# Gate weights split once and kept: a hybrid S5 and RWKV-7 block on one core

## The chip, the cores and the metric

The kernel runs on one core of one Trainium2 chip. The metric is the device time of one execution in microseconds (us). Each execution profiled below has a span (first to last instruction of the program) and a time a little above it. The engines are TensorE (PE in the profile; its weight loads are PEld), VectorE (DVE), ScalarE (ACT), GpSimd (POOL) and SyncE (SP), which here only issues DMAs.

## The reference

One trunk layer on 2048 frames of 1024 features, in float32:

```python
h = rmsnorm(x, norm1_g)
proj = h @ w_in                       # [u | p_rwkv | gate_a | gate_b], 512+1792+1024+1024 columns
gate_a, gate_b = sigmoid(proj[..., s2:s3]), sigmoid(proj[..., s3:])
o_a = s5_branch(u, ...)               # diagonal complex state-space model and half-GLU
o_b = rwkv7_branch(p_rwkv, ...)       # 8 heads x 64, delta-rule recurrence over the frames
merged = gate_a * (o_a @ wb[:512]) + gate_b * (o_b @ wb[512:])
x = x + merged @ w_out
x = x + square(relu(rmsnorm(x, norm2_g) @ w_ff1)) @ w_ff2
return rmsnorm(x, norm_f_g)
```

The change concerns the product of h with the last 2048 columns of w_in, the gate weights.

## The kernel before, in words

Large products are made in three passes (`mm3`, lines 120 to 123): each float32 operand is split into a high part rounded to float32r and a low part, the rest, and TensorE adds high x low, low x high and high x high. The parts come from a copy that rounds (ScalarE as a rule) and a subtraction of the rounded from the raw (GpSimd or VectorE).

The program runs in phases. Phase A makes h, writes its two parts to memory (`h_d`), and projects the RWKV and S5 inputs. Phase B, about 540 to 1400 us, holds two things at once:

- The RWKV recurrence, in 16 chunks of 128 frames: `elem` (elementwise preparation), `inv` (inverse of a triangular matrix per head; its 16 x 16 blocks go through memory in 8 KB transfers, lines 783 to 787, are worked on in the loop of lines 802 to 809 on VectorE, and come back at lines 810 to 816; `X` of line 817 is then what TensorE needs) and `chain` (the state, serial over the chunks).
- `gates`, which makes the gate columns: four quarters `w` of 512 frames; in each the parts of h come from `h_d` (16 tiles, line 969), then 16 strips `m` of 128 columns, 24 matmuls each. `loadw(m)`, called one strip ahead, loads strip m's weights (512 KB, line 955), copies them to the high part `gwh` (ScalarE, line 958) and subtracts to the low part `gwl` (GpSimd, line 959). All this is done anew in each quarter, 64 times in all. The weight tiles alternate between two pools, so a strip's weights lie where those of two strips before lay. The result goes through ScalarE (line 985) and a store that is issued a strip late (line 986) to `gt_d`.

`robin` (line 82) takes a step of `chain`, `gates`, `elem` and `inv` in turn until the chunk's work is done; `gates` goes on into the next chunk. This sets the program order. The framework then orders each engine's instructions by this order and its own model of when each becomes ready, except those pinned with `keep_in_program_order`, and sets the waits. Each engine and each queue of DMA issues runs in the order so found. Nearly all DMAs of phase B are issued by SyncE. `Late` holds back a given number of actions: with `Late()` an action runs when the next one is put.

Phase C (branch outputs, gates applied from `gt_d`, output projection) and phase D (the feed-forward part) follow.

Of the kernel before, what the change touches and what calls it, by code (L numbers as in the profile page):

```python
# [10 lines left out]
F32 = mybir.dt.float32  # L11
# [10 lines left out]
NK = DM // 128  # L22
# [97 lines left out]
def mm3(nc, ps, wh, wl, xh, xl, start, stop):  # L120
    nc.tensor.matmul(ps, wh, xl, start=start, stop=False)  # L121
    nc.tensor.matmul(ps, wl, xh, start=False, stop=False)  # L122
    nc.tensor.matmul(ps, wh, xh, start=False, stop=stop)  # L123
# [473 lines left out]
        weave(dense(), s5_stream(tc, nc, K, io, R, u_d, z_d, sp, pss), ratio=2)  # L597


def phase_b(tc, nc, K, io, pm_d, ob_d, h_d, gt_d, inv_d):  # L600
    V, A, P, T = nc.vector, nc.scalar, nc.gpsimd, nc.tensor
    NS = S // 128
    with ExitStack() as st:
# [343 lines left out]
            D[s] = None  # L947

        def gates():
            late = Late()  # L950

            def loadw(m):
                pool = (gw, gt)[m % 2]
                wr = pool.tile([128, NK, 128], F32, tag="wr", name=f"gwr{m}")
                nc.sync.dma_start(wr, io["win"][18 + m % 16])
                wh = pool.tile([128, NK, 128], F32R, tag="wh", name=f"gwh{m}")
                wl = pool.tile([128, NK, 128], F32R, tag="wl", name=f"gwl{m}")
                A.copy(wh, wr)  # L958
                P.tensor_tensor(wl, wr, wh, op=ALU.subtract)  # L959
                return wh, wl  # L960

            nxt = loadw(0)
            for w in range(NW):
                hs = []
                for k in range(NK):
                    r = []
                    for i in range(2):
                        t = (gw if k < 5 else gt).tile([128, 512], F32R, tag=f"h{i}{k}", name=f"gh{w}_{i}{k}")
                        nc.sync.dma_start(t.bitcast(F32), h_d[i, w, :, k, :])
                        r.append(t)  # L970
                    hs.append(r)
                for _ in range(5):
                    yield
                for m in range(16):
                    wh, wl = nxt
                    j = 16 * w + m
                    if j + 1 < 16 * NW:
                        nxt = loadw(j + 1)
                    pp = psd.tile([128, 512], F32, tag="d", name=f"gp{j}")
                    for k in range(NK):  # L980
                        mm3(nc, pp, wh[:, k], wl[:, k], hs[k][0], hs[k][1], k == 0, k == NK - 1)
                        if k % 2 and k < NK - 1:
                            yield
                    sg = gt.tile([128, 512], F32, tag="sg", name=f"gs{j}", bufs=2)
                    A.copy(sg, pp)
                    late.put(lambda m=m, w=w, sg=sg: nc.sync.dma_start(
                        gt_d[128 * m:128 * m + 128, 512 * w:512 * w + 512], sg))
                    yield
            late.flush()

        gg = Side(gates())
        next(gg)
        for i in range(NS + 2):
# [733 lines left out]
def ff_open(tc, nc, K, io, x1_d, xt_d, r_d, st):  # L1727

    rp = st.enter_context(tc.tile_pool(name="e_r", bufs=1, reuse_waits="tile"))
    s1 = ExitStack()  # L1730
    return s1, FF1(tc, nc, K, io, x1_d, xt_d, r_d, s1, rp)


def phase_d(tc, nc, K, io, x1_d, r_d, out, s1, ff):
    pieces = a_pieces(nc, io, r_d, ff.tile4)
    w2 = {}

    def w2raw(g):
        if g not in w2:
            w2[g] = {}  # L1740
            for j in range(2):
                for l in range(2):
                    t = ff.tile4(2 * j + l, f"w2{g}_{j}{l}")
                    m = 4 * g + 2 * j
                    nc.sync.dma_start(t, io["w2"][m:m + 2, :, 512 * l:512 * l + 512].rearrange("b p n -> p b n"))
                    w2[g][j, l] = t
        return w2[g]

    def start():
        w2raw(0)  # L1750
        for n in range(4):
            pieces[1](n)

    with s1:
        ff.run(s1, start)
    phase_d2(tc, nc, K, io, x1_d, out, pieces, w2raw, ff.tile4)


def setup(tc, nc, st, io):
    K = Net()  # L1760
    cp = st.enter_context(tc.tile_pool(name="glob", bufs=1))
    ca = cp.tile([128, NCST_A], F32, name="csta")
    nc.sync.dma_start(ca, io["cst"][:, 0:NCST_A])
    vec = cp.tile([128, NVEC], F32, name="vec")
    nc.sync.dma_start(vec, io["vec"])
    K.ident = ca[:, 0:128]
    K.r7 = ca[:, 128:144]
    K.mhalf = cp.tile([128, 1], F32, name="mhalf")
    nc.gpsimd.memset(K.mhalf, -0.5)
    K.ss = cp.tile([128, 2, 16], F32, name="ss1")  # L1770
    K.rq = cp.tile([128, 16], F32, name="rq1")
    K.vec = lambda n: vec[:, VOFF[n]:VOFF[n] + VEC_N.get(n, 4)]
    return K
# [34 lines left out]
@with_exitstack  # L1808
def tile_hybrid_block(ctx: ExitStack, tc: tile.TileContext, io: dict, out: bass.AP):
    nc = tc.nc  # L1810
    dp = ctx.enter_context(tc.tile_pool(name="dram", bufs=1, space=DRAM))
    u_d = dp.tile([512, 8, S // 8], F32, name="u_d")
    pm_d = dp.tile([2688, S], F32, name="pm_d")
    gt_d = dp.tile([2 * DM, S], F32, name="gt_d")
    h_d = dp.tile([2, NW, 128, NK, WT], F32, name="h_d")
    inv_d = dp.tile([S // 128, 2, 64, 256], F32, name="inv_d")
    z_d = dp.tile([512, 8, S // 8], F32, name="z_d")
    ob_d = dp.tile([512, S], F32, name="ob_d")
    oa_d = dp.tile([512, S], F32, name="oa_d")
    x1_d = dp.tile([S, DM], F32, name="x1_d")  # L1820
    xt_d = dp.tile([3, 2, 128, 4, 512], F32, name="xt_d")
    r_d = dp.tile([16, 4, 128, 2, 512], F32, name="r_d")
    if True:
        K = setup(tc, nc, ctx, io)
        phase_a(tc, nc, K, io, u_d, pm_d, h_d, z_d)
        phase_b(tc, nc, K, io, pm_d, ob_d, h_d, gt_d, inv_d)
        with ExitStack() as sd:
            ff = []

            def following():  # L1830
                ff.extend(ff_open(tc, nc, K, io, x1_d, xt_d, r_d, sd))
                return ff[1].ahead()

            phase_c(tc, nc, K, io, z_d, oa_d, ob_d, gt_d, x1_d, xt_d, following)
            phase_d(tc, nc, K, io, x1_d, r_d, out, *ff)
# [21 lines left out]
```

## Time and profile before

| | |
|---|---|
| median of 3 runs | 3114.84 us (3110.07 to 3119.49) |
| profiled execution: time, span | 3106.43 us, 3104.7 us |
| mean granted TensorE clock | 0.970 |
| busy of the span: TensorE, VectorE, GpSimd, ScalarE | 94%, 63%, 43%, 38% |
| line 955, loads of raw gate weights | 64 x 512 KB, 3.7 us to landing (median) |
| line 986, stores of gate columns | 64 x 256 KB, 2.8 us to landing (median) |

How to read it: a group's row gives line, engine, operation, what is written and read, the count, then busy us and the mean ns of one, then the engine's idle time before it and what ended that. In a row of waits stand the total us, the number of waits and the longest. In a window's row each engine's busy us is followed by its count of instructions; then come the granted clock, the DMA engines' busy share and GB/s. A tile's or line's row gives minimum/median/maximum in ns, and the first and last start in us. A row in order of time gives start and duration in us, and in brackets the idle time before and what ended it. In instruction names `x<-y` is what is written and what is read. A busy TensorE is not one at its peak, and some matmul records can be missing.

### The profile page before, as it was taken

The page shows a single profiled execution, that of the slowest core. Times are in us where ns is not written, and L with a number is a line of the kernel's source. Part 1 is how long each engine was busy: PE and PEld are TensorE (multiplying, and loading weights), DVE is VectorE, ACT ScalarE, POOL GpSimd, SP SyncE. Part 2 cuts the span into 40 slices and gives each one's busy share as a digit, 9 for nine tenths or more (in the row PEclk, how much of TensorE's full clock was granted, in tenths as well). Part 3 has the DMA queues.
Part 4 walks back from the last instruction along what each step waited for, and adds up shares of the span by engine and source line. Part 5 has one row for each costly group of instructions (what it writes and reads, how often), then busy time and mean ns, then how long its engine had stood idle before and what let it go on. Part 6 is the DMA issues. An engine that isn't in the chain of part 4 may idle for free.

```text
span 3104.7 us, 45582 instructions
## 1 busy us (share of the span) xinstructions
PE 2928.6 (94%) x17024; PEld 2339.1 (75%) x17024; DVE 1942.6 (63%) x3307; ACT 1164.4 (38%) x1843; POOL 1333.7 (43%) x1117
## 2 busy tenths in 40 slices
PE   7989999589899999998999999999999999999998
PEld 5757777367677767777777878887788888888887
DVE  5348875367877777745333266656755566666667
ACT  4441211234343344324444455555333442222233
POOL 3100100645555455422433335555444655555564
PEclk9999999789899999999999999999999999999999
DMA  4344444534435334228656664333533386666664
GB/s 148 96 134 136 137 142 136 180 100 128 127 98 159 92 97 144 77 92 241 194 182 185 197 200 153 109 109 106 176 111 113 97 271 153 151 153 153 154 145 148
DMA packets 320157, 444.10 MB, mean 143 GB/s; under 512 B 112064, under 2 KB 173632, under 8 KB 319936
## 3 DMA queue, kind: packets, MB, share of 16 engines
q1 hardware_dynamic: 291776, 401.34, 40.6%
q0 software_dynamic: 11520, 35.66, 6.7%
q10 hardware_dynamic: 16640, 4.20, 0.5%
q8 instruction: 134, 2.20, 0.3%
q14 instruction: 87, 0.71, 0.1%
HBM read 302.55 MB, written 131.07 MB: 140 GB/s over the span
## 4 chain that ended last, share of the span: by engine, by line
PE 46%; DVE 5%; DMA 4%; issue 2%; POOL 2%; ACT 1%; SPq 0%; POOLq 0%; ACTq 0%; DVEq 0%
PE s L122 6%; PE s L123 6%; PE s L121 6%; PE f L121 5%; PE f L123 5%; PE f L122 5%; DMA wor<-in_wout_dram 1%; DMA g<-gt_d 1%; PE b L121 1%; PE b L122 1%; PE b L123 1%; PE o L121 1%; PE o L122 1%; PE o L123 1%; DVE bl L1318 1%
## 5 line engine op out<-in xcount | busy, mean ns | idle before, releaser
L121 PE MATMUL f<-bl,w1h 128*128 128x512 f32 x896 | 355.5, 397 | 8.9 <-ACT w1h L1345 8.9
L122 PE MATMUL f<-bh,w1l 128*128 128x512 f32 x896 | 351.8, 393 | 3.7 <-POOL w1l L1349 3.7
L123 PE MATMUL f<-bh,w1h 128*128 128x512 f32 x896 | 352.6, 394 | 0.0
L122 PE MATMUL s<-w2h,al 128*128 128x512 f32 x784 | 305.5, 390 | 1.0 <-POOL al L1563 1.0
L123 PE MATMUL s<-w2h,ah 128*128 128x512 f32 x784 | 305.4, 390 | 0.0
L121 PE MATMUL s<-w2l,ah 128*128 128x512 f32 x784 | 305.4, 390 | 0.0
L1349 POOL TENSOR_TENSOR w1l<-w1r,w1h 128x512 fp32r<-128x512 f32 x122 | 174.7, 1434 | 185.1 <-ACT w1h L1345 184.6
L121 PE MATMUL gp<-gh,gwh 128*128 128x512 f32 x512 | 228.8, 447 | 10.9 <-DMA gh<-h_d 10.8
L122 PE MATMUL gp<-gh,gwl 128*128 128x512 f32 x512 | 214.8, 420 | 6.4 <-POOL gwl L959 6.4
L1345 ACT CAST w1h<-w1r 128x512 fp32r<-128x512 f32 x224 | 137.7, 620 | 205.9 <-PE f L123 150.1
L1563 POOL TENSOR_TENSOR al<-ra,ah 128x1024 fp32r<-128x1024 f32 x64 | 167.4, 2617 | 108.0 <-ACT ah L1562 107.8
L123 PE MATMUL gp<-gh,gwh 128*128 128x512 f32 x512 | 211.1, 412 | 0.0
L1593 DVE TENSOR_TENSOR c<-c,s 128x512 f32<-128x512 f32 x224 | 149.9, 684 | 90.2 <-PE s L123 90.0
L121 PEld LDWEIGHTS f<-bl,w1h 128*128 128x128 f32 x896 | 169.8, 190 | 44.8 <-ACT w1h L1345 9.9
L122 PEld LDWEIGHTS f<-bh,w1l 128*128 128x128 f32 x896 | 169.6, 189 | 43.7 <-POOL w1l L1349 7.2
L123 PEld LDWEIGHTS f<-bh,w1h 128*128 128x128 f32 x896 | 169.3, 189 | 38.2
L959 POOL TENSOR_TENSOR gwl<-gwr,gwh 128x1024 fp32r<-128x1024 f32 x64 | 153.7, 2401 | 97.5 <-ACT gwh L958 81.8
L121 PE MATMUL p<-hl,wh 128*128 128x512 f32 x448 | 182.8, 408 | 3.6 <-ACT lo L583 3.6
L123 PE MATMUL p<-hh,wh 128*128 128x512 f32 x448 | 178.5, 399 | 0.0
L122 PE MATMUL p<-hh,wl 128*128 128x512 f32 x448 | 178.1, 398 | 0.0
L122 PEld LDWEIGHTS s<-w2h,al 128*128 128x128 f32 x784 | 147.3, 188 | 31.7 <-POOL al L1563 1.4
L123 PEld LDWEIGHTS s<-w2h,ah 128*128 128x128 f32 x784 | 147.3, 188 | 30.5
(382 smaller groups left out, 6995.1 us busy)
## 6 DMA issues: line engine op xcount, KB each, us to landing
gwr<-in_win_dram SPq DMA_DIRECT2D x64, 512.0 KB, 3.7
w1r<-in_w_dram SPq DMA_DIRECT2D x64, 512.0 KB, 3.4
r_d<-c SPq DMA_DIRECT2D x128, 256.0 KB, 2.0
ra<-r_d SPq DMA_DIRECT2D x64, 512.0 KB, 3.5
ch<-r_d POOLq DMA_DIRECT2D x42, 512.0 KB, 5.8
gh<-h_d SPq DMA_DIRECT2D x64, 256.0 KB, 5.0
gt_d<-gs SPq DMA_DIRECT2D x64, 256.0 KB, 2.8
g<-gt_d SPq DMA_DIRECT2D x64, 256.0 KB, 3.4
```

The source lines that it names most:

```text
L121: nc.tensor.matmul(ps, wh, xl, start=start, stop=False)
L122: nc.tensor.matmul(ps, wl, xh, start=False, stop=False)
L123: nc.tensor.matmul(ps, wh, xh, start=False, stop=stop)
L959: P.tensor_tensor(wl, wr, wh, op=ALU.subtract)
L1318: V.tensor_tensor(l[k], o, h[k], op=ALU.subtract)
L1345: cast = A.copy(h, o)
L1349: (P if n % 2 or edge else V).tensor_tensor(l, o, h, op=ALU.subtract)
L1563: P.tensor_tensor(l, raw[n], h, op=ALU.subtract)
L1593: V.tensor_tensor(d, d, bank, op=ALU.add if i in (4, 5, 6) else ALU.subtract)
```

## The change

In the first quarter, as before, each strip's weights are loaded raw and split. Now both parts are also stored to a new tensor in memory, `gs_d` (16 strips x 2 parts x 512 KB), one strip late; the last strip's at the last strip of the quarter. In the other three quarters both parts are loaded from `gs_d` straight into the tiles that the matmuls read, with no copy and no subtraction. The values are the same bits.

```diff
-def phase_b(tc, nc, K, io, pm_d, ob_d, h_d, gt_d, inv_d):
+def phase_b(tc, nc, K, io, pm_d, ob_d, h_d, gt_d, gs_d, inv_d):
...
         def gates():
-            late = Late()
+            late, keep = Late(), Late()
 
             def loadw(m):
+
                 pool = (gw, gt)[m % 2]
-                wr = pool.tile([128, NK, 128], F32, tag="wr", name=f"gwr{m}")
-                nc.sync.dma_start(wr, io["win"][18 + m % 16])
                 wh = pool.tile([128, NK, 128], F32R, tag="wh", name=f"gwh{m}")
                 wl = pool.tile([128, NK, 128], F32R, tag="wl", name=f"gwl{m}")
+                if m >= 16:
+                    for e, t in enumerate((wh, wl)):
+                        nc.sync.dma_start(t.bitcast(F32), gs_d[m % 16, e])
+                    return wh, wl
+                wr = pool.tile([128, NK, 128], F32, tag="wr", name=f"gwr{m}")
+                nc.sync.dma_start(wr, io["win"][18 + m])
                 A.copy(wh, wr)
                 P.tensor_tensor(wl, wr, wh, op=ALU.subtract)
+
+                def store():
+                    for e, t in enumerate((wh, wl)):
+                        nc.sync.dma_start(gs_d[m, e], t.bitcast(F32))
+
+                keep.put(store)
                 return wh, wl
...
                     j = 16 * w + m
+                    if j == 15:
+                        keep.flush()
                     if j + 1 < 16 * NW:
                         nxt = loadw(j + 1)
...
+    gs_d = dp.tile([16, 2, 128, NK, 128], F32, name="gs_d")
...
-        phase_b(tc, nc, K, io, pm_d, ob_d, h_d, gt_d, inv_d)
+        phase_b(tc, nc, K, io, pm_d, ob_d, h_d, gt_d, gs_d, inv_d)
```

## The prediction, made before the changed kernel was run

> **What bounds the kernel now.** I read the stage table first (busy time of each engine in chosen stretches), then the list of waits on TensorE, then the groups of VectorE instructions, and last the order of time around single stalls. The edited code runs in one stage, from 540 to 1400 us. There TensorE works through 64 gate strips (24 matmuls each), four quarters of 16, woven with the RWKV recurrence. The edit spares work in quarters two to four, 760 to 1400 us, and adds stores in the first, 540 to 760 us.
>
> ```profile
> core 0: us, PE busy (x) PEld busy (x) DVE busy (x) ACT busy (x) POOL busy (x), PEclk, DMA share, GB/s
> 540.00:760.00 220.00, 171.01 (x1440) 132.35 (x1439) 129.58 (x228) 69.55 (x113) 125.64 (x138) 0.85 0.44 133
> 760.00:1400.00 640.00, 591.99 (x5973) 460.02 (x5971) 457.23 (x833) 235.58 (x380) 304.76 (x309) 0.94 0.38 113
> 1700.00:1800.00 100.00, 100.00 (x460) 82.71 (x459) 30.67 (x43) 44.32 (x82) 37.01 (x30) 1.00 0.63 195
> ```
>
> In quarters two to four TensorE is busy 592 of 640 us and its granted clock is 0.94, against 1.00 in a later stage without stalls. So 48 us are idle, and 6% of 640, 38 us, is clock not granted. ScalarE and GpSimd are half idle or more; sparing them time is worth nothing by itself. What TensorE waits for is this:
>
> ```profile
> engine line waited for: us in total, times, longest us
> PE P L667 <- DVE X L817: 14.4, 5, 5.2
> PE bo L745 <- DVE ys L944: 11.7, 3, 4.6
> PE U L899 <- DVE Rs L895: 8.1, 4, 4.5
> ...
> PE gp L122 <- POOL gwl L959: 0.6, 1, 0.6
> ```
>
> The gate weights themselves make TensorE wait 0.6 us (the last row). The other three rows, 34.2 us, are waits for VectorE, and nearly all of the small rows left out are too (46 us with them). So the question is why VectorE is late, and whether the removed work has a part in it. It has:
>
> ```profile
> 921.86 4.42 DVE L934 TENSOR_TENSOR ys<-ys,y 128x512 f32<-128x512 f32 x1
> ...
> 922.12 2.38 POOL L959 TENSOR_TENSOR gwl<-gwr,gwh 128x1024 fp32r<-128x1024 f32 x1
> 924.47 1.26 POOL L746 TENSOR_TENSOR BK<-km,e 128x512 f32<-128x512 f32 x1
> ...
> 929.84 1.44 PE L667 MATMUL P<-X,TM 64*64 64x64 f32 x22 [5.19 <-DVE X L817]
> ...
> 927.00:933.80 6.80, 3.96 (x37) 3.28 (x37) 5.69 (x7) 1.57 (x3) 4.54 (x3) 0.50 0.82 231
> ...
> L934 DVE TENSOR_TENSOR ys<-ys,y x14: 645/693/4420, 780.0 to 1385.3; 128x512 f32<-128x512 f32 x14
> ```
>
> The VectorE multiply at L934 has a median of 0.69 us. Beside the gate weights' subtraction on GpSimd (L959) and the next GpSimd operation it took 4.42 us and ended when the second did. The X of L817 behind it came late, TensorE waited 5.19 us for it, and its clock stood at 0.50 for 6.8 us (last window row). That is one case; groups and both ends of the list show how common it is:
>
> ```profile
> L805 DVE TENSOR_TENSOR yt<-NC,YC 64x15 f32<-64x15 f32 (+7 forms) x195 | 70.2, 360 | 13.6 <-DMA NC<-inv_d 8.3
> L807 DVE TENSOR_TENSOR YC<-YC,yt 64x15 f32<-64x15 f32 (+7 forms) x195 | 56.6, 290 | 5.7
> L934 DVE TENSOR_TENSOR ys<-ys,y 128x512 f32<-128x512 f32 x14 | 18.9, 1354 | 0.3
> L717 DVE TENSOR_TENSOR AR<-rm,e 128x512 f32<-128x512 f32 x11 | 17.0, 1547 | 9.3 <-ACT e L706 9.1
> ...
> L805 DVE TENSOR_TENSOR yt<-NC,YC x195: 116/206/2841, 765.1 to 1343.8; 64x15 f32<-64x15 f32 x26, 64x28 f32<-64x28 f32 x26, 64x39 f32<-64x39 f32 x26, 64x48 f32<-64x48 f32 x26
> L807 DVE TENSOR_TENSOR YC<-YC,yt x195: 101/206/2392, 765.3 to 1344.0; 64x15 f32<-64x15 f32 x26, 64x28 f32<-64x28 f32 x26, 64x39 f32<-64x39 f32 x26, 64x48 f32<-64x48 f32 x26
> L717 DVE TENSOR_TENSOR AR<-rm,e x11: 647/694/6431, 759.5 to 1241.3; 128x512 f32<-128x512 f32 x11
> ...
> 765.97 2.30 DVE L805 TENSOR_TENSOR yt<-NC,YC 64x39 f32<-64x39 f32 x1
> 765.85 2.37 POOL L959 TENSOR_TENSOR gwl<-gwr,gwh 128x1024 fp32r<-128x1024 f32 x1
> ...
> 1341.45 2.35 DVE L807 TENSOR_TENSOR YC<-YC,yt 64x28 f32<-64x28 f32 x1
> 1341.37 2.39 POOL L959 TENSOR_TENSOR gwl<-gwr,gwh 128x1024 fp32r<-128x1024 f32 x1 [3.15 <-ACT gwh L958]
> ```
>
> Mean minus median, times count: L805 (360-206) x 195 = 30.0 us, L807 16.4, L934 9.3, L717 9.4: 65 us of VectorE time lost beside GpSimd. 22 VectorE instructions, the first and the last of them in the four rows above, were each stretched by at least 1.8 us beside one L959. So L959's share is at least 22 x 1.8 = 40 us, at most these 65 and what smaller groups add.
>
> **The change part by part.** The profiled execution took 3106.4 us; the median of the runs, 3114.84, is 8.4 above it. I work out a difference and apply it to both.
>
> Removed in quarters two to four, 48 times each: the ScalarE copy, the GpSimd subtraction and the 512 KB load of raw weights.
>
> ```profile
> L958 ACT CAST gwh<-gwr x64: 1027/1049/1069, 548.6 to 1389.4; 128x1024 fp32r<-128x1024 f32 x64
> L959 POOL TENSOR_TENSOR gwl<-gwr,gwh x64: 2332/2380/2850, 549.7 to 1390.5; 128x1024 fp32r<-128x1024 f32 x64
> L955 SPq DMA_DIRECT2D gwr<-in_win_dram x46: 328/351/1654, 789.3 to 1377.6; - x46
> DMA to landing us min/median/max: 3.1/3.8/5.6
> ```
>
> *ScalarE*: 48 x 1.05 = 50 us of an engine busy 236 of 640; I count nothing. *GpSimd*: 48 x 2.38 = 114 us off, and with it the 40 to 65 us of VectorE. What TensorE gets of that: I followed the unbroken run of VectorE work back from each of the 21 stalls of 0.4 us or more that VectorE ended between 760 and 1400 us, and took, stall by stall, the smaller of the stall and the time stretched beside L959 in that run. It sums to 33 us. The stalls at 1307.72 (2.51 us) and 1352.76 (2.27 us) get nothing: the run ahead of them is short and begins at a transfer's landing. Bounds: 0, if other waits fill the place, and all 46 us. I take 33.
>
> *The clock*: 38 us not granted follow such stalls. With 33 of 47 us of stalls gone I take 70% back, 27 us, and 0.6 of that as work really paced by the clock (the rest is small matmuls and idle time): 16 us. Bounds 0 and 38.
>
> *Added in the first quarter*: 32 stores of 512 KB, from SyncE's queue. No row has such a store; the 256 KB ones of L986 issue in 0.34 us and land in 2.5, so 32 x 0.34 = 11 us of queue time, on an engine that mostly waits. Bounds 0 to 11; I take 3, since each is issued a strip late and GpSimd has ended by then; behind it stand the small transfers of the inverse.
>
> *Added afterwards*: two 512 KB loads per strip in place of one, and a new wait: they write where strip m-2's weights lie, so SyncE waits for that strip's last matmul. Now it waits only for L959, and loads far ahead:
>
> ```profile
> 799.75 0.35 SPq L955 DMA_DIRECT2D gwr<-in_win_dram  x1
> 812.51 0.34 SPq L986 DMA_DIRECT2D gt_d<-gs  x1
> ...
> 811.90 0.59 ACT L985 COPY gs<-gp 128x512 f32<-128x512 f32 x1 [0.54 <-PE gp L123]
> ...
> 1394.40 0.59 ACT L985 COPY gs<-gp 128x512 f32<-128x512 f32 x1 [3.95 <-issue]
> 1399.84 0.59 ACT L985 COPY gs<-gp 128x512 f32<-128x512 f32 x1 [4.85 <-PE gp L123]
> ...
> SPq L986 <- ACT gs L985: 132.0, 30, 11.1
> SPq L955 <- POOL gwl L959: 86.4, 31, 7.8
> ```
>
> The load of strip 20 went out at 799.75, 12 us before strip 17 ended (its L985 copy is at 811.90). The edited load can go out only at the end of strip 18. SyncE already waits there 30 times for the copy that follows the same matmul (L986, 132 us), and the instruction order is planned anew by the framework's own model of readiness, so I expect the new wait beside that one and L955's 86 us gone. The pair of loads then has one strip's time to land: between 3.8 us (both at once) and 0.35 + 2 x 3.8 = 8.0 (one after the other). A strip takes 640/48 = 13 us on average, but the last, without recurrence beside them, 5.4 (1394.40 to 1399.84). Some four short strips could be late by up to 2.6 us: 0 to 10 us, I take 3. By the Trainium skill ("DMA: Bandwidth & Descriptors", section Bandwidth) a 1 MB load takes 6.15 us, which would make it 3 us by an estimate; no run here shows the pair yet.
>
> *Small transfers*: the inverse's 8 KB transfers share the queue with the loads.
>
> ```profile
> L814 SPq DMA_DIRECT2D Y<-inv_d x104: 313/429/1032, 778.9 to 1350.0; - x104
> ```
>
> 104 of them are 13 chunks of eight. An extra load issued ahead costs 0.35 us and some data time; bounds 0 and one extra microsecond on each of 13 chunks; I take 5.
>
> Sum: -33 - 16 + 3 + 3 + 5 = -38 us. 3106.4 becomes 3068 for the profiled execution, 3114.8 becomes 3077 for the median.
>
> **The rivals.**
> *Hidden.* VectorE is freed and only waits longer for TensorE and for the inverse's round trip. For it: the two stalls without any stretched work, 2.4 us each. If each of 13 chunks keeps such a stall, 31 of 47 us remain, 16 go, the clock gives nothing, costs 11: -5, 3110. Against it: most stalls have 2 us or more of stretched work just ahead.
>
> *Slower.* SyncE's queue: the gate loads wait for the strip's end, and the inverse's transfers (L783, L810, L814), ready by then, stand behind them; VectorE's chain gets its blocks late and TensorE waits for X. The nearest price is L986's wait, 132/30 = 4.4 us. Once in each of 13 chunks: +57 - 38 = +19, 3134. It decides from 38/13 = 2.9 us a chunk. Against it: the L986 wait is in the queue already.
>
> *More.* All 46 us of VectorE stalls go and 0.6 of the 38 us of clock, with 5 of costs: -64, 3051. A rule speaks for it: the Trainium skill ("TensorE: Matmul & The Clock Gate", section HAM oscillation) asks only that no idle gap exceed about 3.4 us, so short stalls that are left would cost no clock. The rows disagree:
>
> ```profile
> 1051.91 0.80 PE L667 MATMUL P<-X,TM 64*64 64x64 f32 x20 [1.79 <-DVE yt L805]
> ...
> 1053.30:1056.70 3.40, 3.40 (x37) 2.49 (x35) 2.09 (x10) 0.39 (x1) 0.00 (x0) 0.50 0.00 1
> ```
>
> A stall of 1.79 us was followed by 3.4 us at half clock.
>
> **How the numbers follow.** Forecast 0.61, hidden 0.15, slower 0.12, more 0.12. The forecast's own range, from the bounds of the clock, the costs and a new instruction order, is 3055 to 3105. The 8-in-10 range takes in most of the other cases: 3046 to 3118. About 0.3%, 9 us, is what a measurement can tell from no change. Faster than that: nearly all of forecast and more, and a quarter of hidden: 0.75. Slower 0.12. Within: 0.13.
>
> **What would show it.** In the changed trace: L805 and L807 means near 0.25 us from 760 us on; TensorE's waits for VectorE there near 14 us and its clock near 0.98; the stage some 40 us shorter, everything after it the same length. Wrong if SyncE's waits for TensorE come to stand ahead of L783 or L810, if TensorE waits for the loaded weights in more than a few strips, or if VectorE's means stay up because other GpSimd work moves into the freed time.

## The result, and the profile after

The changed kernel takes 3074.93 us (median of 4 runs, 3067.89 to 3079.11) against 3115.95 us of the kernel before (3110.07 to 3119.49): a ratio of 0.9873, 95% interval 0.9852 to 0.9894, 41 us less by the medians. A second set of runs on another occasion gave 3075.24 us and 0.9877 [0.9852, 0.9902]. The profiled execution took 3079.11 us, its span is 3077.3 us and its mean granted clock 0.979.

The stage table of the kernel after, as it was read before (busy us and counts of each engine, then clock, DMA share, GB/s):

```profile
core 0: us, PE busy (x) PEld busy (x) DVE busy (x) ACT busy (x) POOL busy (x), PEclk, DMA share, GB/s
540.00:760.00 220.00, 165.46 (x1308) 124.23 (x1307) 129.79 (x218) 64.91 (x105) 112.52 (x120) 0.86 0.63 199
760.00:1365.00 605.00, 580.83 (x6101) 451.49 (x6100) 400.72 (x843) 195.69 (x342) 201.16 (x278) 0.99 0.55 165
```

From 760 us to the end of the stage TensorE is idle 24 us where it was 48, and its clock is 0.99 where it was 0.94. The first stretch went the other way: 165 us busy against 171, and the DMA engines 0.63 against 0.44 of the time.

The ends of strips are the copies from `gp`. ScalarE's order of time, the kernel before first (end of the first quarter; that of the last strip, 1399.84, stands in the prediction), then the kernel after (end of the first quarter and of the last):

```profile
773.54 0.58 ACT L985 COPY gs<-gp 128x512 f32<-128x512 f32 x1 [0.70 <-PE gp L123]
```

```profile
781.81 0.58 ACT L998 COPY gs<-gp 128x512 f32<-128x512 f32 x1 [0.70 <-PE gp L123]
...
1364.32 0.59 ACT L998 COPY gs<-gp 128x512 f32<-128x512 f32 x1 [6.54 <-PE gp L123]
```

Quarters two to four took 1399.84 - 773.54 = 626.3 us before and 582.5 after, 44 less. The first quarter, from the first gate matmul (557.1 and 556.6), took 216.4 and now 225.2 us, 9 more. What follows the last strip took 1704.8 us to the end of the span and now 1713.0; in the second profile of the kernel after it took 1709.7, and between 1705.6 and 1712.2 in the eleven other versions below, whose later phases are the same code, so that part is scatter of single executions. These three lengths are the yardstick of all the experiments:

| kernel | first quarter | quarters two to four | rest | median us | ratio to before [95%] |
|---|---|---|---|---|---|
| before | 216.4 | 626.3 | 1704.8 | 3115.95 | |
| after | 225.2 | 582.5 | 1713.0 | 3074.93 | 0.9873 [0.9852, 0.9894] |
| after, second set | 226.3 | 578.9 | 1709.7 | 3075.24 | 0.9877 [0.9852, 0.9902] |
| dummy subtraction | 225.5 | 635.4 | 1706.7 | 3132.54 | 1.0073 [1.0046, 1.0101] |
| writes only, before | 216.5 | 566.7 | 1709.4 | 3048.47 | 0.9794 [0.9768, 0.9820] |
| one read each, before | 211.4 | 626.2 | 1707.7 | 3107.32 | 0.9996 [0.9981, 1.0011] |
| writes only, after | 232.7 | 600.0 | 1709.4 | 3097.99 | 0.9958 [0.9940, 0.9976] |
| two stores | 216.3 | 577.8 | 1705.6 | 3056.73 | 0.9823 [0.9799, 0.9848] |
| stores on other queues | 223.7 | 578.2 | 1712.2 | 3074.85 | 0.9881 [0.9861, 0.9900] |
| loads twice | 227.3 | 644.1 | 1708.5 | 3142.69 | 1.0091 [1.0068, 1.0113] |
| third pair of tiles | 226.8 | 582.3 | 1710.2 | 3079.11 | 0.9900 [0.9878, 0.9921] |
| loads on ScalarE's queue | 220.5 | 627.4 | 1709.3 | 3117.89 | 1.0023 [1.0004, 1.0042] |
| split in phase A | 193.9 | 576.3 | 1710.4 | 3105.26 | 0.9980 [0.9962, 0.9999] |
| low part only | 209.3 | 572.4 | 1711.3 | 3046.62 | 0.9790 [0.9770, 0.9811] |

The two profiles of the kernel after differ by 1 us in the first quarter and by 4 in the other three. Another instruction order moves the first quarter further: it takes 211 to 217 us in the versions that store nothing or next to nothing there, and 220 to 233 in those with 32 stores from SyncE's queue. Smaller differences say nothing.

What TensorE waits for in the kernel after, from 760 us to the end of the stage, its longest rows:

```profile
PE m L667 <- DVE TM L777: 5.3, 3, 2.5
PE gp L122 <- DMA gwl<-gs_d: 3.6, 2, 2.4
PE gp L121 <- DMA gh<-h_d: 2.6, 2, 2.2
PE gp L121 <- DMA gwh<-gs_d: 2.3, 2, 1.6
PE U L899 <- DVE Rs L895: 1.9, 4, 0.8
PE P L667 <- DVE X L817: 1.8, 2, 1.6
```

X of L817, which cost 14.4 us, costs 1.8; all waits for VectorE together, with the small rows, are 12 us instead of 46. New are two rows of waits for the loaded weights, 5.9 us. VectorE's groups from 760 us, and then the row of L805 with minimum/median/maximum:

```profile
L805 DVE TENSOR_TENSOR yt<-NC,YC 64x15 f32<-64x15 f32 (+7 forms) x195 | 46.7, 239 | 17.3 <-DMA NC<-inv_d 12.2
L807 DVE TENSOR_TENSOR YC<-YC,yt 64x15 f32<-64x15 f32 (+7 forms) x195 | 44.0, 225 | 5.4
L934 DVE TENSOR_TENSOR ys<-ys,y 128x512 f32<-128x512 f32 x14 | 10.0, 716 | 0.2
```

```profile
L805 DVE TENSOR_TENSOR yt<-NC,YC x195: 101/205/1299, 774.0 to 1309.8; 64x15 f32<-64x15 f32 x26, 64x28 f32<-64x28 f32 x26, 64x39 f32<-64x39 f32 x26, 64x48 f32<-64x48 f32 x26
```

The median of L805 is what it was, near 205 ns; the mean fell from 360 to 239 and the longest from 2841 to 1299; L934's mean fell from 1354 to 716. The long ones are gone, not the work.

### The profile page after: what moved, and what is told of

Its sections match the earlier page's. It is cut to its first block, busy times and chain, and to the rows that moved or that the text cites. A ratio compares the mean times of both kernels' runs of the same rounds, so it can differ in the third digit from the quotient of the medians.

```text
span 3077.3 us, 45569 instructions
## 1 busy us (share of the span) xinstructions
PE 2913.9 (95%) x17024; PEld 2322.5 (75%) x17024; DVE 1892.2 (61%) x3307; ACT 1119.9 (36%) x1795; POOL 1219.9 (40%) x1069
## 4 chain that ended last, share of the span: by engine, by line
PE 54%; DVE 10%; DMA 6%; issue 5%; POOL 3%; ACT 2%; SPq 1%; POOLq 0%; DVEq 0%; ACTq 0%
PE s L121 6%; PE s L123 6%; PE s L122 6%; PE f L121 5%; PE f L123 5%; PE f L122 5%; PE gp L121 2%; PE gp L122 2%; PE gp L123 2%; DMA g<-gt_d 1%; PE o L121 1%; PE o L122 1%; PE o L123 1%; DVE YC L807 1%; DVE bl L1331 1%
## 5 line engine op out<-in xcount | busy, mean ns | idle before, releaser
L121 PE MATMUL gp<-gh,gwh 128*128 128x512 f32 x512 | 222.4, 434 | 22.3 <-DMA gh<-h_d 13.5
L123 PE MATMUL gp<-gh,gwh 128*128 128x512 f32 x512 | 209.6, 409 | 0.0
L121 PEld LDWEIGHTS s<-w2l,ah 128*128 128x128 f32 x784 | 147.6, 188 | 33.6 <-ACT s L1599 3.0
```

## The experiments

**The theories.** Theory A is the prediction's: a VectorE instruction with two operands in SBUF is held up while GpSimd's subtraction reads SBUF, the recurrence behind it is late, TensorE waits, and its clock drops after the wait. The rivals: the gain comes from something else that the edit took away or moved (the ScalarE copies, the order of the instructions, other waits); or it is GpSimd's being busy at all, not its reading. A second question is where the part of the gain went that the kernel after doesn't show: into the stores, the loads, or the late weights.

**1. The subtraction put back beside the loads.** The changed kernel with a subtraction of the two loaded parts into the tile that is otherwise unused; nobody reads its result.

```diff
                         nc.sync.dma_start(t.bitcast(F32), gs_d[m % 16, e])
+                    wx = pool.tile([128, NK, 128], F32R, tag="wr", name=f"gwx{m}")
+                    P.tensor_tensor(wx, wh, wl, op=ALU.subtract)
                     return wh, wl
```

> The changed kernel, and in quarters two to four GpSimd again makes a subtraction of the old shape, high minus low part, into a tile that nothing reads. The planned order of TensorE, ScalarE and SyncE is the same as in the changed kernel, instruction for instruction. Theory A (VectorE is held up while GpSimd's subtraction reads its two operands): nearly all of the gain goes again, 3105 to 3118 us; L805's mean after 760 us back at 0.33 to 0.36 us, TensorE's waits for VectorE back at 35 to 46 us. Theory B (the gain comes from GpSimd's queue being emptier): also back near 3110. Theory C (the gain comes from the new instruction order or from ScalarE's copies being gone): stays at 3070 to 3080.

ScalarE's and SyncE's instructions stand in exactly the order of the kernel after, TensorE's in the same planned order; on VectorE two are moved. In this kernel, the stage window, VectorE's group, one pair of instructions in order of time, and TensorE's longest wait:

```profile
760.00:1365.00 605.00, 551.76 (x5712) 427.28 (x5712) 444.39 (x828) 186.74 (x324) 305.20 (x320) 0.96 0.50 150
```

```profile
L805 DVE TENSOR_TENSOR yt<-NC,YC 64x15 f32<-64x15 f32 (+7 forms) x195 | 69.4, 356 | 14.5 <-DMA NC<-inv_d 9.3
```

```profile
1047.98 2.40 POOL L961 TENSOR_TENSOR gwx<-gwh,gwl 128x1024 fp32r<-128x1024 f32 x1 [1.85 <-DMA gwl<-gs_d]
...
1048.02 2.42 DVE L805 TENSOR_TENSOR yt<-NC,YC 64x48 f32<-64x48 f32 x1
```

```profile
PE P L667 <- DVE X L817: 13.9, 6, 4.6
```

Quarters two to four took 635.4 us, 53 more than in the kernel after; L805's mean is 356 ns again, the X wait 13.9 us. The L805 beside the subtraction took 2.42 us and ended with it, where its median is 0.2. Nothing but the subtraction was added, in an order all but unchanged, so the gain is the subtraction's absence. It does bring a wait of its own: GpSimd stands 104 us for the loads that its subtractions read. But VectorE waits for GpSimd only 5 us longer than in the kernel after (14.8 against 10.1 us), so GpSimd's being late is not what brings the 53 us back. The whole kernel became slower than before, 1.0073: with the subtraction back, the loads and stores of the change are pure cost. That the subtraction is the cause is shown here; that it acts by reading is the next question.

**2. Writes in place of the subtraction, in the kernel before.** In quarters two to four GpSimd writes zeros to the low part twice, reading nothing. The low part is left out there. No load or store is added.

```diff
-                P.tensor_tensor(wl, wr, wh, op=ALU.subtract)
+                if m < 16:
+                    P.tensor_tensor(wl, wr, wh, op=ALU.subtract)
+                else:
+                    for _ in range(2):
+                        P.memset(wl.bitcast(F32), 0.0)
```

> The kernel before, where in quarters two to four GpSimd fills the low part with zeros, twice, in place of the subtraction; ScalarE's copies, the single load, the waits of the matmuls on GpSimd and nearly the whole order stay as before (the low part of the gate weights is left out). Theory A: the gain is there without any of the new loads or stores: 3062 to 3080 us, L805's mean 0.24 us. Theories B and C: 3108 to 3120, as before.

The GpSimd instructions, VectorE's group and the stage window (of which some us at the end lie behind the last strip, this stage being shorter):

```profile
L963 POOL MEMSET gwl<- x96: 944/952/1061, 765.7 to 1332.0; 128x1024 f32 x96
```

```profile
L805 DVE TENSOR_TENSOR yt<-NC,YC 64x15 f32<-64x15 f32 (+7 forms) x195 | 46.0, 236 | 19.7 <-DMA NC<-inv_d 14.4
```

```profile
760.00:1365.00 605.00, 587.78 (x6077) 458.84 (x6074) 415.54 (x855) 251.03 (x405) 285.42 (x360) 0.99 0.45 129
```

GpSimd still works 96 x 0.952 = 91 us on the weights where the subtractions took 114, and in the same strips; ScalarE's copies and the raw loads are as before. Quarters two to four took 566.7 us: the gain from this cause alone is 626.3 - 566.7 = 59.6 us. TensorE's waits for VectorE there are 12 us. Of the instructions of L805 and L807, 77 ran beside one of these writes and no other GpSimd work, and 75 of them took their usual time; in the kernel before 18 ran so beside a subtraction, and 13 were stretched. So it isn't GpSimd's being busy as such, nor ScalarE's copies. The zeros are also what TensorE multiplies here, but the kernel after reaches the same clock, 0.99, and the same 12 us of waits with the real weights.

**3. One tile read, in the kernel before.** As experiment 2, with two instructions that read one tile. The low part is a scaled copy of the raw weights there, not the rest of the rounding.

```diff
-                        P.memset(wl.bitcast(F32), 0.0)
+                        P.tensor_scalar(wl, wr, 2.0 ** -11, None, op0=ALU.mult)
```

> This is the kernel before with the subtraction of the second, third and fourth quarter replaced by two GpSimd instructions that each read one tile (the raw weights times a constant) and write the low part; the low part is thus a scaled copy of the weights there. No new load or store. It stands beside the version in which the two instructions only wrote zeros, whose quarters two to four took 566.7 us against 626.3 before. Theory A, VectorE's instructions with two SBUF operands are held while GpSimd reads SBUF: GpSimd reads nearly all the time again, so most of the gain is gone; quarters two to four 600 to 640 us, L805 at a mean of 0.30 to 0.36 us, VectorE's stalls of TensorE 30 to 50 us there, time 3085 to 3120 us. Rival, it is not GpSimd's reading but something else that the version with zeros changed (zeros as data of TensorE, a lighter instruction): quarters two to four 560 to 580 us, L805 at 0.23 to 0.25 us, time 3040 to 3065 us.

The GpSimd instructions, one pair in order of time, a wait of VectorE's and one of TensorE's:

```profile
L963 POOL TENSOR_SCALAR gwl<-gwr x93: 2761/2771/3215, 772.1 to 1387.1; 128x1024 fp32r<-128x1024 f32 x93
```

```profile
1335.10 2.77 POOL L963 TENSOR_SCALAR gwl<-gwr 128x1024 fp32r<-128x1024 f32 x1
...
1335.11 1.10 DVE L807 TENSOR_TENSOR YC<-YC,yt 64x64 f32<-64x64 f32 x1
```

```profile
DVE e L697 <- POOL cmid L695: 15.8, 8, 3.1
...
PE P L667 <- DVE X L817: 17.3, 6, 6.0
```

The sum came out as theory A said: 626.2 us for the three quarters, ratio 0.9996, the whole gain gone. The way there did not. L805's mean was 264 ns, not the 300 to 360 expected, since beside an instruction that reads one tile a VectorE instruction was held for a part of the other's 2.77 us only: the L807 above took 1.10 us where 0.21 is the median, the longest L807 1.29. There are twice as many GpSimd instructions, and L807's mean is 304 ns, above the 292 of the kernel before. GpSimd, at 2.77 us instead of 0.95, is itself late: VectorE waits 15.8 us for L695, a wait of 5.4 in the kernel before's stretch of 773 to 1400 us. It also waits 24.2 us for the inverse's transfer NC, where it was 6.3. So reading stretches VectorE here too, in smaller portions, but part of this kernel's loss is a busier GpSimd, and the parts were not told apart. It supports experiment 2 without being a clean mirror of it.

**4. Writes in place of the subtraction, in the changed kernel.** As 1, with two writes of zeros in place of the subtraction.

```diff
-                    P.tensor_tensor(wx, wh, wl, op=ALU.subtract)
+                    for _ in range(2):
+                        P.memset(wx, 0.0)
```

> As the run before, but GpSimd fills the unread tile with zeros, twice, in place of the subtraction: about as long on GpSimd, but it reads nothing. Theory A: the gain stays, 3070 to 3083 us, L805's mean 0.24 us. Theory B: the gain goes in the measure of GpSimd's time, 3095 to 3112. Theory C: 3070 to 3080.

It took 600.0 us for the three quarters, in between. The writes depend on no load, and all 96 of them ran between 746.8 and 886.4 us, not strip by strip, so they don't stand in for the subtraction; experiment 2, in which each stands where the subtraction stood, replaced this run. It does show where the loss lies: the second quarter, with the writes in it, is 19 us longer than in the kernel after (215.9 against 197.2), the third and fourth are as long within 2 us. There the writes, back to back, held an instruction that neither theory had named. VectorE's L942 reads one large tile only, and its median is 0.34 us:

```profile
795.07 5.41 POOL L962 MEMSET gwx<- 128x1024 f32 x6
...
796.57 4.05 DVE L942 TENSOR_SCALAR ys<-ys,vec 128x128 f32<-128x128 f32 x2
```

Two of them ended with the last of six writes, the longer of the two after 3.98 us. So writing alone holds this instruction, though not those of L805 and L807. How much of the 19 us that is was not measured.

**5. Two stores in place of 32.** Only strip 0 is stored, and every strip loads that; the weights of the other strips are left out in the last three quarters.

```diff
-                        nc.sync.dma_start(t.bitcast(F32), gs_d[m % 16, e])
+                        nc.sync.dma_start(t.bitcast(F32), gs_d[0, e])
...
-                keep.put(store)
+                if m == 0:
+                    keep.put(store)
...
-                    if j == 15:
+                    if j == 1:
```

> The changed kernel with the stores of strip 0 alone; all later quarters load strip 0's parts for every strip (so other strips' weights are left out). Loads and waits as in the changed kernel, 30 of 32 stores gone. If the stores cost the 9 us by which the first quarter grew (225.2 against 216.4 us): 3064 to 3069 us, first quarter 214 to 219 us. If the growth came from the new order: 3072 to 3079, first quarter 222 to 227.

The first quarter took 216.3 us, as in the kernel before. The 32 stores thus cost some 9 us where I had taken 3. (The whole kernel gained more, a ratio of 0.9823 against 0.9873; the rest is spread over the later parts, where single profiles scatter by as much.) The stores in the kernel after, and one of TensorE's waits from 540 to 760 us there:

```profile
L968 SPq DMA_DIRECT2D gs_d<-gwh x16: 319/376/985, 571.9 to 757.4; - x16
L968 SPq DMA_DIRECT2D gs_d<-gwl x16: 319/346/645, 572.4 to 759.8; - x16
...
DMA to landing us min/median/max: 2.6/3.8/9.3
```

```profile
PE gp L121 <- ACT gwh L963: 6.4, 3, 4.9
```

They take 32 x 0.36 = 12 us to issue and up to 9.3 to land. A wait of TensorE for ScalarE's copy of the weights, 6.4 us, is new: the kernel before has none, and this experiment 0.6 us. Its longest part, in the kernel after, in TensorE's, ScalarE's and SyncE's rows:

```profile
663.23 0.80 PE L121 MATMUL gp<-gh,gwh 128*128 128x512 f32 x1 [4.95 <-ACT gwh L963]
...
662.15 1.03 ACT L963 CAST gwh<-gwr 128x1024 fp32r<-128x1024 f32 x1
...
631.49 0.98 SPq L968 DMA_DIRECT2D gs_d<-gwh  x1
...
652.77 0.43 SPq L962 DMA_DIRECT2D gwr<-in_win_dram  x1
...
SPq L810 <- DVE YC L807: 24.3, 3, 11.2
```

One might think that the copy of strip m has to wait until strip m-2's high part, whose place it takes, is stored. This case says otherwise: the copy is strip 8's, and strip 6's high part, issued at 631.49, had landed 24 us before. What came late is strip 8's raw load, issued at 652.77 and landed at 659.12, after SyncE had stood 11.2 us for VectorE's YC. Whether the stores put it there isn't shown, and what makes up the 9 us is open.

**6. Stores issued by other engines.** High parts from ScalarE's queue, low parts from GpSimd's.

```diff
-                    for e, t in enumerate((wh, wl)):
-                        nc.sync.dma_start(gs_d[m, e], t.bitcast(F32))
+                    nc.scalar.dma_start(gs_d[m, 0], wh.bitcast(F32))
+                    nc.gpsimd.dma_start(gs_d[m, 1], wl.bitcast(F32))
```

> The changed kernel, with the stores issued by the engines that make the parts: the high one by ScalarE, the low one by GpSimd, so that SyncE waits for neither. If the first quarter's 9 us come from SyncE standing in wait before the stores (56 us of such waits there): first quarter 216 to 220 us, ratio to before 0.984. If they come from the data or from the tiles being held until they are stored: 223 to 227, ratio 0.987.

The first quarter took 223.7 us, all but 2 us of the 9 still there: SyncE's issue time, which was the prediction's term for the stores, is at most a small part of what they cost here. The wait for ScalarE's copy is not among TensorE's listed waits in this kernel, and the quarter is as long without it.

**7. Each part loaded twice.** The second load goes to the unused tile.

```diff
+                    wx = pool.tile([128, NK, 128], F32, tag="wr", name=f"gwx{m}")
+                    for e in range(2):
+                        nc.sync.dma_start(wx, gs_d[m % 16, e])
```

> The changed kernel, and each of the 96 loads of quarters two to four is made a second time into a tile that nothing reads. The three quarters of the changed kernel are 16 us longer than those of the kernel before with the write-only fill (582.5 against 566.7 us). If that is the price of the loads' traffic beside the inverse's small transfers, it comes once more: 592 to 605 us, ratio 0.991 to 0.995. If it is the late start of the loads at the strip's end: 580 to 588, ratio 0.987 to 0.989.

The inverse's last transfers (Y, line 814) in the kernel after, then the same and the stage window with loads twice:

```profile
L814 SPq DMA_DIRECT2D Y<-inv_d x104: 302/429/1712, 784.8 to 1316.8; - x104
...
DMA to landing us min/median/max: 1.7/1.9/4.1
```

```profile
DMA to landing us min/median/max: 1.7/3.1/5.1
```

```profile
760.00:1365.00 605.00, 554.62 (x5575) 429.12 (x5575) 379.83 (x796) 183.37 (x318) 193.23 (x273) 0.92 0.70 223
```

The three quarters are 62 us longer, far above either expectation, and the clock falls to 0.92, with VectorE's means low (L805 243 ns). But this is not the price of the loads' traffic alone. Both extra loads go to one tile, so the second waits for the first, and SyncE, whose queue the inverse's transfers share, stands for it (from the end of the first quarter to that of the last):

```profile
SPq L962 <- DMA gwx<-gs_d: 102.1, 31, 5.7
```

Nor is the later landing of Y, a median of 1.2 us, the price: from the issue of YC (line 810) to the last landing of Y it takes a median of 7.5 us here as in the kernel after. How the 62 us divide between traffic and SyncE's wait is open. With the change's own loads the median landing of Y is 1.9 us against 1.8 before: as far as the median shows, these loads are near free for the inverse.

**8. A third pair of tiles.** The loaded parts alternate over three pairs and are loaded two strips ahead.

```diff
+                if m >= 16:
+                    a, b, c, d = ((gw, "wr", gt, "wr"), (gw, "wh", gw, "wl"), (gt, "wh", gt, "wl"))[(m - 16) % 3]
...
-                    if j + 1 < 16 * NW:
-                        nxt = loadw(j + 1)
+                    for n in range(j + 1 + len(nxt), min(j + (3 if j >= 15 else 2), 16 * NW)):
+                        nxt.append(loadw(n))
```

> The changed kernel with a third pair of weight tiles in quarters two to four (the raw tiles, idle there), so that each strip's loads go out a whole strip earlier. If late loads are what the three quarters still lose: TensorE's waits for loaded weights, 5.9 us, go to zero, the three quarters 566 to 575 us, ratio 0.982 to 0.985. If the loads' traffic is it: 578 to 585, ratio 0.986 to 0.988.

TensorE's waits for the loaded weights are gone from the list, and the three quarters take 582.3 us, as in the kernel after. So taking away the 5.9 us of late weights gains nothing that can be seen; what is waited for in their place was not followed.

**9. Loads on ScalarE's queue.**

```diff
-                        nc.sync.dma_start(t.bitcast(F32), gs_d[m % 16, e])
+                        nc.scalar.dma_start(t.bitcast(F32), gs_d[m % 16, e])
```

> The changed kernel, with the 96 loads of quarters two to four issued by ScalarE, whose queue carries nothing else there; bytes and times of need are the same. If the 10 us that these quarters are longer than with the low part alone loaded (582.5 against 572.4 us) come from the pair of loads in SyncE's queue, ahead of the inverse's small transfers: 570 to 576 us, the small transfers' landing at 1.8 us again, ratio to before 0.982 to 0.985. If they come from traffic in the shared engines or from the order: 579 to 586, landing 1.9 to 2.1 us, ratio 0.987 to 0.990.

The transfer that takes the inverse's blocks back to memory (YC, line 810), from 760 to 1400 us, in the kernel after and then here, where TensorE's longest wait follows:

```profile
L810 SPq DMA_DIRECT2D inv_d<-YC x13: 451/451/452, 782.7 to 1310.4; - x13
...
DMA to landing us min/median/max: 1.9/1.9/3.2
```

```profile
DMA to landing us min/median/max: 1.9/3.4/5.6
```

```profile
PE P L667 <- DVE X L817: 27.4, 10, 4.8
```

The whole gain is lost, 627.4 us, which neither expectation had. SyncE has less to do, and yet its small transfers land later. From YC's issue to the last landing of Y it takes a median 10.9 us here, 7.5 in the kernel after and 7.2 before; 13 chunks x 3.4 = 44 us, about what the stage lost against the kernel after (45). This is the outcome of the "slower" rival (the blocks come late and TensorE waits for X), with a price just above the 2.9 us at which it decides, and the kernel ends just above the time before, at 1.0023. It is not that rival's mechanism: the rival had the small transfers stand behind the loads in SyncE's queue, and here the loads are in another. In the change as made it doesn't occur.

**10. The split done in phase A.** All 16 strips are split in four pieces each and their low parts stored during phase A; phase B loads raw weights and low parts in all four quarters, as in 11.

```diff
+            for q in range(4):
+                ks = slice(2 * q, 2 * q + 2)
+                wh = wp.tile([128, 2, 128], F32R, tag="gwh", name=f"gwh{g}_{q}", bufs=1)
+                nc.scalar.copy(wh, wr[:, ks])
+                nc.gpsimd.tensor_tensor(wl[:, ks], wr[:, ks], wh, op=ALU.subtract)
+            nc.sync.dma_start(gs_d[g, 1], wr)
...
+                    if gates and (w == 2 or (w == 0 and mi in (4, 8, 12))):
+                        split_gate(gates.pop(0))
```

> The low parts of all 16 strips are made and stored in phase A, in pieces, where GpSimd is 10% busy; phase B loads them in all four quarters and makes the high parts on ScalarE from the raw weights. GpSimd's last 16 subtractions (38 us) leave phase B. Theory A: the first quarter falls from 209 to 190 to 200 us, since GpSimd was 95% busy or more at its start; phase A, where TensorE waited for nothing from 300 us on, stays at 557 to 562: ratio to before 0.972 to 0.977. Rival: VectorE in phase A, 75 to 80% busy, is held up in turn and TensorE waits there: phase A 565 to 580, ratio 0.977 to 0.985.

The first quarter fell to 193.9 us, as it should if its subtractions have their price too; since it also starts later, beside other work of the recurrence, the length alone doesn't show it. Phase A gave more back, and more than the rival had: the first gate matmul comes 76 us later, at 633.6. Its last part, 300 to 540 us, in the kernel before and then here, with two of TensorE's waits up to 633 us:

```profile
300.00:540.00 240.00, 237.56 (x1114) 184.34 (x1113) 177.18 (x432) 46.20 (x70) 25.82 (x28) 0.99 0.45 138
```

```profile
300.00:540.00 240.00, 212.15 (x956) 163.17 (x955) 160.08 (x374) 51.53 (x94) 49.50 (x58) 0.94 0.45 141
```

```profile
PE p L121 <- DVE lc L569: 17.6, 2, 12.8
...
PE py L268 <- DVE X L403: 9.0, 2, 7.4
```

TensorE had been busy 99% there. Now it waits for VectorE, and its clock is 0.94. The work was moved from beside one VectorE chain to beside another. But held VectorE instructions are the smaller part of the 76 us: beside the pieces of the split, 34 were stretched, by 14 us in all. TensorE also waits 10 us for the ScalarE and GpSimd instructions of lines 516 and 517, and its first gate matmul waits 20.65 us for `h_d`, where it was 9.1. The parts were not told apart.

**11. Only the low part kept.** The raw weights are loaded and copied to the high part in all quarters, as before; only the low part is stored and loaded.

```diff
-                if m >= 16:
-                    for e, t in enumerate((wh, wl)):
-                        nc.sync.dma_start(t.bitcast(F32), gs_d[m % 16, e])
-                    return wh, wl
...
                 A.copy(wh, wr)
+                if m >= 16:
+                    nc.sync.dma_start(wl.bitcast(F32), gs_d[m % 16, 1])
+                    return wh, wl
...
-                    for e, t in enumerate((wh, wl)):
-                        nc.sync.dma_start(gs_d[m, e], t.bitcast(F32))
+                    nc.sync.dma_start(gs_d[m, 1], wl.bitcast(F32))
```

> The changed kernel, but only the low part is stored and loaded; the high part is made anew by ScalarE from the raw weights in every quarter. GpSimd's 48 subtractions are gone as in the changed kernel, ScalarE's 48 copies (50 us) are back, 16 of 32 stores are gone, and half of the loads can go out early again. Theory A (VectorE held up beside the subtraction is the whole gain): at least the changed kernel's ratio to before, 0.983 to 0.987, the first quarter 219 to 222 us, the other three together 572 to 583. Rival (ScalarE's spared time has a part in it): 0.988 to 0.992, the three quarters 585 to 600.

This is the best version: 3046.62 us, 0.9790 [0.9770, 0.9811], with nothing left out. The 48 ScalarE copies are back, and cost nothing that can be seen. Half the stores are gone, and the first quarter is 16 us shorter (209.3 against 225.2). The stores can't be all of that, since it is also 7 us shorter than in the kernel before, which has none; the order of the instructions differs too, and the rest is not explained; the three other quarters took 572.4 us, for the same bytes loaded as in the kernel after. TensorE's waits for the weights are not in its list: the raw load goes out early again, since a ScalarE copy frees its tile, and only one 512 KB load is left that has to wait until strip m-2 is done.

**12. The changed kernel again.** No edit.

> The changed kernel once more, beside the other two on one chip. Ratio 0.985 to 0.990; the time after the last gate strip, 1713.0 us in its first profile against 1704.8 before, is expected at 1704 to 1712 if that difference is chance, and at 1713 or above if it belongs to the change.

The second set of the table: 226.3 and 578.9 us, and the same ratio within 0.0004.

## Why the prediction was right

The time, 3075 us against 3077 predicted, and the sign were right. Its terms were less exact, and that the time came so close is luck, since their errors cancelled: the spared subtraction gave 59.6 us and not 49, the added transfers cost 21 to 25 and not 11, which leaves 35 to 39 where I said 38.

**Stalls and clock (-33 and -16).** The mechanism held (experiments 1 and 2), and so did the readings it named: means of 239 and 225 ns for L805 and L807 where I said near 250, 12 us of TensorE's waits for VectorE where I said 14, a clock of 0.979 where I said 0.98. The size was too small: 49 predicted, 59.6 measured in experiment 2. Giving nothing for the stalls at 1307.72 and 1352.76 was not the error, as about as much wait is left as I left. The clock was: in experiment 2 as in the kernel after it went from 0.94 to 0.99, that is from 38 us not granted to 6, so 32 us came back where I took 27, and my discount of 0.6 on it was from no row. 34 us of stalls gone and all 32 of clock would make 66, above the 59.6; a factor of 0.8 would fit, which is a fit to one number and not a finding.

**Stores (+3).** They cost 9 (experiment 5). The bounds of 0 to 11 held it, the reason did not: I priced SyncE's issue time, and moving the issue to other engines left 7 of the 9 (experiment 6). The prediction named the inverse's small transfers behind the stores; it had no term for the raw loads of the next strips, one of which came late (experiment 5), whether or not through the stores. What the 9 us are made of stays open.

**Loads (+3 late, +5 small transfers).** Against experiment 2, which has no added transfers, the kernel after's three quarters are 12 to 16 us longer in its two profiles; I took 8. Late weights showed as forecast, in a few strips, 5.9 us with the longest at 2.4 where I allowed 2.6. But a third pair of tiles takes those waits away and the stage stays as long (experiment 8), so lateness isn't the price. What the 12 to 16 us are stays open: YC lands as before, Y 0.1 us later in the median. Low parts alone, with the same bytes, cost 6 us, little more than the 4 us by which the two profiles of the kernel after differ.

**The landing of the pair.** I put it between 3.8 and 8.0 us. The loads of line 959, and SyncE's longest wait, in the kernel after:

```profile
L959 SPq DMA_DIRECT2D gwl<-gs_d x48: 319/410/1481, 772.1 to 1353.5; - x48
L959 SPq DMA_DIRECT2D gwh<-gs_d x48: 319/376/931, 772.5 to 1352.5; - x48
...
DMA to landing us min/median/max: 3.2/4.6/8.6
...
SPq L959 <- PE gp L123: 123.8, 32, 13.5
```

One load takes a median of 4.6 us. From the first issue of a pair to its second landing it is 5.6 us, between the two bounds; six of the 48 pairs took over 8.0, where I had put the upper one. The new wait for a strip's last matmul took the place of the old ones as said: 123.8 us here, where L986 had 132 and L955 86.

**The rivals.** "Hidden" fell: VectorE did not just wait longer elsewhere, as 34 of its 46 us of stalls left TensorE. "Slower" did not occur in the change; experiment 9 has its outcome, by another way. "More" fell too: it took away all 46 us of stalls, and 12 were left, near the 14 of my forecast. Its gross gain was 69 (46 and 0.6 of 38), mine 49, and the measured 59.6 lies between; the time, 3075, lies by mine. The rule on idle gaps that spoke for it did not hold. One of the stalls left in the kernel after, and the clock soon after it:

```profile
1193.66 0.37 PE L667 MATMUL m<-AR,BK 64*128 64x128 f32 x1 [2.46 <-DVE TM L777]
```

```profile
1195.55:1198.96 3.41, 3.41 (x45) 3.07 (x44) 0.56 (x1) 0.51 (x1) 1.61 (x4) 0.50 1.05 347
```

A gap of 2.46 us, the longest from a VectorE wait in these quarters, was followed by 3.4 us at half clock. The Trainium skill ("TensorE: Matmul & The Clock Gate", section HAM oscillation) asks that gaps stay below about 3.4 us; this trace doesn't agree, the gap here is shorter and the clock fell all the same.

**The rest of the span** was forecast unchanged. By the profiles it may be up to 8 us longer, and the scatter of the versions covers that. It is why the profiled execution missed its own forecast, 3079 us against 3068, by more than the median did.

## What to carry to other kernels

An engine with idle time can still set the pace by what it reads: before moving or sparing work on GpSimd, compare mean with median of VectorE's instructions with two operands, and look for the long ones beside a GpSimd instruction that reads. What such work costs is both the stalls of the bounding engine and the clock that it loses after them; here that was 59.6 us where VectorE's own lost time was put at 40 to 65. The place that the work goes to has a chain too (experiment 10), and here the version that spared the work with fewer stores (low parts only) was better than keeping everything. Before large loads go to another queue to spare the small urgent transfers, try it: here that made the small ones late (experiment 9).

## What the runs showed of the hardware

A VectorE instruction of 0.2 us with two SBUF operands took up to 2.4 us beside a GpSimd subtraction of two tiles, ending with it; up to 1.3 us (L807's longest) beside a GpSimd instruction that reads one tile, which itself goes on to 2.77 us; and it was not held by one that only writes: in experiment 2, 75 of 77 L805 and L807 beside a write alone took their usual time, and the other two, 0.69 us at most, stood behind an L942 that was itself held. The Trainium skill ("SBUF — State Buffer", section Who interferes with whom) says that a VectorE instruction with two SBUF inputs contends with a GpSimd instruction that reads SBUF and not with one that only writes it. The first two experiments agree, with 53 and 60 us. The section also calls the shared port pair an exclusive lock; beside the instruction that reads one tile, VectorE instructions were not held to its end: of 62 that took over 0.1 us more than the median of their kind, none lost more than 1.5 of its 2.77 us, and the measurement decides.

Three things I had not expected. VectorE's L942, which reads one large tile, was held by GpSimd's writes, up to 3.98 us where its median is 0.34 (experiment 4). The GpSimd instruction that reads one tile takes longer, 2.77 us, than the subtraction that reads two, 2.38. And a transfer of 64 KB issued from SyncE's queue landed later with large loads on another engine's queue (YC's median 3.4 us) than with the same loads in its own (1.9).
